# Grouped-query scores with each head's keys standing twice: two full-height products per block

## The chip, the cores and the metric

The kernel runs as one launch on one core of one Trainium2 chip. The metric is device time in microseconds (us); lower is better. Times of several runs are compared by their median, and one further execution was taken with the hardware profiler.

## What is computed

Two layers of a hybrid trunk are run for two groups of tokens with shared weights: 128 context tokens, and 256 latent tokens that also read a cache of 128 context keys. Each layer mixes tokens in three branches (grouped-query attention, latent attention, a recurrent block), merges them by gates and an output projection, and ends in a convolutional feed-forward part. The part that matters here, cut from the reference:

```
qa = rmsnorm(qa.reshape(B, T, H_A, HD_A), lp['g_qa'])     # 8 heads of 64
ka = rmsnorm(ka.reshape(B, T, KV_A, HD_A), lp['g_ka'])    # 2 heads of 64
if cache is not None:                                     # latent tokens
    qa, ka = axial_rope(qa, ang_a), axial_rope(ka, ang_a)
    ka_all = jnp.concatenate([ck, ka], axis=1)            # 128 cached keys, 256 own
...
s = jnp.einsum('bqkgd,bskd->bkgqs', qblk, k, preferred_element_type=jnp.float32) * scale
p = jax.nn.softmax(s, axis=-1).astype(v.dtype)
return jnp.einsum('bkgqs,bskd->bqkgd', p, v)
```

Everything is float32. The kernel gets that precision from a faster matmul type by splitting an operand into a high part (`hi`, rounded to that type) and a low part (`lo`, the rest) and adding the products hi hi, hi lo and lo hi.

## The kernel before

All 384 tokens (128 context, 256 latent) go through a layer together, as three tiles of 128 tokens. `layer_items` writes out by hand, layer by layer, a list of items; an item is one step of TensorE with at most one unit of weights (128 rows by up to 1024 columns). The weights stream through a ring: SP's queue loads a unit into `RAW`, ScalarE writes its high part to `WH`, VectorE the low part to `WL`, and the item's products use both. The order of the items in a layer is: keys and values (`kva`), queries (`qa`), eight steps of the recurrent branch (`xr`, `yr`, `gl`, `wg`), latent attention's projections (`ckr`, `qb`), the recurrent projection (`oc`), `uv` and `uk`, then gates with the two attention projections (`gl`, `oa`, `ob`), in layer 0 with units of the modulation spread among them, then `out`, the feed-forward part (`gat`, `val`, `dn`) and further modulation. An `xr`, `yr` or `gl` item has 24 products of 384 columns.

Work that isn't tied to an item is put on a list `side` of small steps with a budget each; every item pops some of them (`BUDGET`). The eight grouped-query heads are a list of events (`events_a`), of which two are taken behind each `oc` item (`EVENTS`): scores of a head, normalisation, transposes of the probabilities, and for every second head the product with the values. `events_b` does the same for the latent heads among the `gl`, `oa` items.

The instructions so taken down are not issued in that order. `Plan` notes for each what it has to wait for, prices it (`cost`; a product by its columns, whatever its rows), and a list scheduler makes the order of each engine in up to 12 sweeps. Each engine then runs its instructions in that order. All are issued from one line, L371, so the profile's rows carry that line and have to be told apart by tile and shape. `FA` is a float32 area, `RA` the area of the split operands, `PS` the eight PSUM banks.

Keys of the grouped-query heads (`kt`, one side step of a layer, behind the last `kva` item): `KA[:, t]` holds 128 tokens by two key heads of 64. Three transposes put both heads below each other into bank 6 (head 0 in rows 0 to 63, head 1 in rows 64 to 127). Together with the cached keys (`CKC`, loaded already transposed into `FA`) they are written to `KAH` (high part, both heads) and to `KAX[0]` and `KAX[1]`: `KAX[g]` has the low part in the rows of head g and a copy of the high part of the same head in the other 64 rows. Bank 6 is later one of the seven that the `xr`, `yr`, `gl` and `wg` items take in turn; the fourth of those items takes it.

Queries (`q` in `events_a`): for a pair of heads a tile `QTH` or `QTL` holds for one head the high part in that head's 64 rows and the low part in the other 64.

Scores of a head (`s(n)`, `att_scores`): three blocks of queries by keys, 128x384, 128x128 and 128x384, in banks 3 and 4. Each is a sum of two products that are issued next to each other: one over the head's 64 rows (hi hi) and one over all 128 rows (hi lo and lo hi at once). So a head has six products, of alternating height. The latent heads use three products of 96 rows for each block (`mm3`) instead.

Of the kernel before, what the change touches and what calls it, by code (L numbers as in the profile page):

```python
# [14 lines left out]
D = 1024  # L15
# [4 lines left out]
NT = 384                    # columns: 128 context tokens, 256 latent tokens  # L20
TOK = (0, 128, 256)         # first column of each token tile
SEQS = ((0, 128), (128, 256))  # first column and length of each sequence
# [4 lines left out]
WIDTH = 1024                # columns of a weight unit  # L27
NRAW, NW = 4, 4             # units loaded, units split
NPEND = {"out": 8, "dn": 4}  # units whose products wait for the last of them and then go tile by tile
# [4 lines left out]
# per-feature parameters, one column per 128 features  # L34
# [16 lines left out]
# ---------------------------------------------------------------- order of the weights  # L51
QUARTERS = ("q0", "q1", "q2", "q3")     # parts of the first modulation, by features
NARROW = QUARTERS + ("g0", "g1", "h0", "h1")   # parts of 512 columns; halves of the first gate, quarters of the second modulation
# [5 lines left out]
ADDED = ((0, 'g0'), (0, 'g1'), (0, 'h0'), (0, 'h1'), (0, 'm2b'), (1, 'm1a'), (1, 'm1b'), (1, 'gt1'), (1, 'm2b'))   # (layer, part) whose products are added up before the sum over the partitions  # L59
# [9 lines left out]
def fill(items, extra):  # L69
    """extra spread evenly over items"""  # L70
    out, n, k = [], len(items), 0
    for i, it in enumerate(items):
        out.append(it)
        while k < len(extra) and (k + 1) * n <= (i + 1) * len(extra):
            out.append(extra[k])
            k += 1
    return out + extra[k:]
# [11 lines left out]
def layer_items(l):  # L89
    """Every entry is one step of the tensor engine with at most one unit of weights, in order."""  # L90
    more = l + 1 < DEPTH
    s = [("kva", l, k) for k in range(2)] + [("qa", l, k) for k in range(4)]
    if l == 0:                                                  # half of the features while the other's modulation is on its way
        s = ada(0, "q0") + [("norm1", 0, 0)]
        for q in range(1, 4):
            b = ada(0, QUARTERS[q])
            s += [("kva", 0, q - 1)] + b[:2] + [("qa", 0, q - 1)] + b[2:] + [("norm1", 0, q)]
        s += [("kva", 0, 3), ("qa", 0, 3)]
# [57 lines left out]
# ---------------------------------------------------------------- the order of the instructions  # L156
# [4 lines left out]
class Plan:  # L161
    """Takes down instructions in an order that is right, and hands them to the engines in one that keeps them busy.

    An instruction comes behind those whose results it reads, and those whose operands or results it overwrites.
    Of the others an engine gets the one that is waited for soonest; the order in which the tensor engine's were
    taken down sets the pace."""
# [18 lines left out]
    # ---- taking down  # L185
    @staticmethod
    def spans(ap):
        """[(first, last word)] and the partitions that an access pattern covers"""
# [41 lines left out]
    def add(self, eng, method, f, args, kw):  # L230
# [20 lines left out]
        if tab:                                                 # the functions that need a table stay in order  # L251
# [14 lines left out]
    def depend(self, op, outs, ins):  # L266
        before = {}
        for write, aps in ((False, ins), (True, outs)):
            for ap in aps:
                self.touch(op.i, ap, write, before)  # L270
                if ap.space == bass.MemoryType.PSUM:            # the engines take turns at a bank
# [6 lines left out]
        if op.eng == "PE":                                      # accumulations of a bank stay in order  # L278
# [6 lines left out]
    def join(self):  # L285
        """what is taken down inside goes to its engine in one piece"""
# [5 lines left out]
    def touch(self, me, ap, write, before):  # L292
        """notes what ap covers; before[op]: whether me has to wait for op's end"""
# [16 lines left out]
    # ---- handing out  # L310
    def lag(self, p, s):
        """from the end of p to the first start of s"""
# [6 lines left out]
    def sweep(self, rank, back):  # L319
        """starts of all instructions, each engine taking the ready one of the lowest rank; in reversed time if back"""  # L320
# [27 lines left out]
    def order(self):  # L348
        ops = self.ops
        now, rank = 0.0, [None] * len(ops)  # L350
        for op in ops:                                          # the pace of the tensor engine
            if op.eng == "PE":
                rank[op.i] = now
                now += op.dur
# [23 lines left out]
# ---------------------------------------------------------------- the kernel  # L378
def trunk(tc, I, O, depth=DEPTH):
    nc = tc.nc  # L380
    with tc.tile_pool(name="sb", bufs=1) as sb, tc.tile_pool(name="ps", bufs=1, space=bass.MemoryType.PSUM) as pp:
        def t(name, shape, dtype=F32):
# [7 lines left out]
            NST=t("NST", [16]), SM=t("SM", [256]), XS=tc.dram_tile([3, 128, D], F32, name="x_spill"),  # L390
# [8 lines left out]
def _emit(plan, G, V, A, PE, SP, I, O, depth, B):  # L399
    PS, FA, RA, HH, HL, RAW, WH, WL = (B[k] for k in ("PS", "FA", "RA", "HH", "HL", "RAW", "WH", "WL"))  # L400
    PARM, PAR, GV, CST, CS, MOD, GEV, RG, NST, SM, XS, AS, ONE = (
        B[k] for k in ("PARM", "PAR", "GV", "CST", "CS", "MOD", "GEV", "RG", "NST", "SM", "XS", "AS", "ONE"))
# [22 lines left out]
    # ---- addresses  # L425
# [8 lines left out]
    KAH, KAX = ra(9264, 512), [ra(9776 + 512 * i, 512) for i in range(2)]  # L434
# [16 lines left out]
    CKC = fa(11286, 128)  # L451
# [48 lines left out]
    def rsq_few(v, n):  # L500
        """v ** -0.5 for a few columns"""
# [15 lines left out]
    # ---- the stream of weights  # L517
# [7 lines left out]
    spare = {}                                                  # places of split units beside the ring's  # L525
# [50 lines left out]
    def on_gpsimd(u):  # L576
        """units that are split where VectorE is behind"""
# [22 lines left out]
    def take():  # L600
        """the next unit: (hi, lo), or what was loaded for one that isn't split"""
# [46 lines left out]
    # ---- constants  # L648
# [20 lines left out]
    def rnn_constants():  # L669
# [4 lines left out]
        # z = exp(-|lam|): 2 ** -k times a series  # L674
# [16 lines left out]
        # log1p(z) = 2 atanh(z / (2 + z))  # L691
# [14 lines left out]
    # ---- modulation  # L706
# [89 lines left out]
    def alpha_build(l, which):  # L796
        """AL[:, i] = 32 (gate_i + bias) g_post, on all partitions"""
# [11 lines left out]
    # ---- norms  # L809
# [3 lines left out]
    def rstd(ss, eps):  # L813
        """(D * (mean + eps)) ** -0.5 from the sums of two halves"""
# [35 lines left out]
    def post_half(t, h, ss):  # L850
        """what half of out needs before its norm is known"""
# [9 lines left out]
    # ---- token-major projections of attention  # L861
# [12 lines left out]
    def headnorm(banks, dst, heads, g):  # L874
        """steps to dst[t] = rmsnorm of the first heads*64 columns of each bank, rotated for the latents"""
# [40 lines left out]
    # ---- attention  # L916
# [42 lines left out]
    def heads(q, s, pv, per):  # L959
        """steps of the eight heads, each between two items"""  # L960
# [17 lines left out]
    def events_a():  # L978
        def q(p):
# [3 lines left out]
            for q, h, o in ((QTH[p % 2], LOW, HIGH), (QTL[p % 2], HIGH, LOW)):   # hi in the head's rows, lo in the other's  # L983
# [4 lines left out]
        def s(n):  # L988
            q, h = ((QTH, LOW), (QTL, HIGH))[n % 2]
            q, x = q[(n // 2) % 2], KAX[n % 2]  # L990

            def product(out, q0, k0, w):                                # hi hi, then hi lo and lo hi in one
                with plan.join():
                    PE.matmul(out, lhsT=q[h, q0:q0 + 128], rhs=KAH[h, k0:k0 + w], start=True, stop=False)
                    PE.matmul(out, lhsT=q[:, q0:q0 + 128], rhs=x[:, k0:k0 + w], start=False, stop=True)
# [15 lines left out]
    # ---- recurrent branch  # L1011
    def tap(y, b, w, d):
        """adds w times the column d further on, within each sequence"""
# [70 lines left out]
    # ---- the walk over the items  # L1084
# [11 lines left out]
    def require(key):  # L1096
        """the step of that name is behind us"""
# [11 lines left out]
    def do(it):  # L1109
# [29 lines left out]
        elif kind == "kva":  # L1139
            k0 = it[2]  # L1140
            if k0 == 0:
# [3 lines left out]
                SP.dma_start(out=CKC, in_=I["ckT"][l])  # L1145
# [6 lines left out]
            if k == KD - 1:  # L1152
# [4 lines left out]
                def kt():  # L1157
                    for t in range(3):
                        PE.transpose(PS[:, 6, 128 * t:128 * t + 128], KA[:, t], IDN)
# [407 lines left out]
```

## Time and profile before

| what | value |
|---|---|
| time, median of 3 runs | 1491.57 us |
| the three runs | 1489.84, 1491.57, 1496.32 us |
| span of the profiled execution | 1487.3 us |
| TensorE products (PE), busy | 1441.8 us, 97% |
| TensorE weight loads (PEld), busy | 1322.3 us, 89% |
| VectorE (DVE), busy | 1089.1 us, 73% |
| ScalarE (ACT), busy | 823.5 us, 55% |
| GpSimd (POOL), busy | 89.4 us, 6% |
| granted TensorE clock, mean | 0.991 of full speed |
| read from memory | 219.40 MB, 150 GB/s over the span |

The span runs from the first to the last instruction of the profiled execution; the profile gives no other time of that execution. Busy times of the engines overlap. TensorE's products are pipelined: the profile's duration of one (0.33 us for 384 columns) holds its whole way through the array, so the distance from one start to the next is what a product costs in a stream. Rows with the operation LDWEIGHTS, engine PEld, are the loads of the stationary operand that precede each product. Shapes such as 64*128 64x384 mean: a stationary operand of 64 rows by 128 columns, a moving one of 64 rows by 384 columns.

### The profile page before, as it was taken

Reading aid. Unit: us, or ns where it says so; the run is one execution under the profiler, and the core shown is the slowest. Engines: PE = TensorE matmul, PEld = TensorE weight load, DVE = VectorE, ACT = ScalarE, POOL = GpSimd, SP = SyncE. Lnnn points to the kernel's source line nnn. Section 1 sums busy time; section 2 is a strip of 40 time slices with the busy share of each in tenths; the row PEclk is TensorE's granted clock in tenths of the full one; section 3 lists DMA queues with packets and bytes.
Section 4 is the critical chain, followed back from the end, with each engine's and each line's share of the span. In section 5 each row is a group of like instructions: output and inputs, shape, how many; then the busy total and the mean of one; then the engine's idle time right before and its main releaser. Section 6 shows DMA issues by size and latency. Waiting matters only on the chain.

```text
span 1487.3 us, 22398 instructions
## 1 busy us (share of the span) xinstructions
PE 1441.8 (97%) x8408; PEld 1322.3 (89%) x8408; DVE 1089.1 (73%) x2150; ACT 823.5 (55%) x1450; POOL 89.4 (6%) x70
## 2 busy tenths in 40 slices
PE   7999999999898999999989999999999999999998
PEld 5999988988786999997769999979999879999886
DVE  3989896898586798988768787966556477777533
ACT  4689965766335554452255799646544455454321
POOL 0000000334002000000020000000000200000000
PEclk9999999999999999999999999999999999999999
DMA  9433331445674554547754333412246364433341
GB/s 362 165 122 121 122 124 53 131 170 160 214 262 170 172 193 147 173 153 251 243 205 137 124 121 110 127 59 75 87 148 206 126 205 124 127 125 126 128 128 57
DMA packets 79101, 225.11 MB, mean 151 GB/s; under 512 B 9808, under 2 KB 21648, under 8 KB 78992
## 3 DMA queue, kind: packets, MB, share of 16 engines
q1 hardware_dynamic: 68576, 216.04, 43.6%
q10 hardware_dynamic: 10416, 7.64, 2.0%
q8 instruction: 66, 1.08, 0.3%
q14 instruction: 43, 0.35, 0.1%
HBM read 219.40 MB, written 4.24 MB: 150 GB/s over the span
## 4 chain that ended last, share of the span: by engine, by line
PE 85%; DVE 5%; DMA 5%; issue 2%; ACT 1%; ACTq 0%; SPq 0%; POOL 0%; DVEq 0%; POOLq 0%
PE PS L371 85%; DMA RAW<-in_wstream_dram 4%; DVE FA L371 3%; DVE WL L371 1%; ACT FA L371 1%; DMA FA<-in_wstream_dram 0%; ACT WH L371 0%; DMA a_spill<-FA 0%; DVE SM L371 0%; DVE RA L371 0%; ACTq L371 0%; SPq L371 0%; POOL SM L371 0%; ACT RA L371 0%; DVE MOD L371 0%
## 5 line engine op out<-in xcount | busy, mean ns | idle before, releaser
L371 DVE TENSOR_TENSOR WL<-RAW,WH 128x1024 fp32r<-128x1024 f32 (+4 forms) x318 | 351.3, 1107 | 173.1 <-ACT WH L371 172.1
L371 ACT ACTIVATE WH<-RAW 128x1024 fp32r<-128x1024 f32 (+3 forms) x328 | 311.3, 954 | 261.3 <-PE PS L371 218.2
L371 PE MATMUL PS<-HH,WH 128*128 128x384 f32 x1344 | 452.7, 337 | 0.5 <-DVE FA L371 0.4
L371 PE MATMUL PS<-HL,WH 128*128 128x384 f32 x1344 | 450.0, 335 | 0.8 <-DVE HL L371 0.8
L371 PE MATMUL PS<-HH,WL 128*128 128x384 f32 x1344 | 449.8, 335 | 0.0
L371 PEld LDWEIGHTS PS<-HH,WH 128*128 128x128 f32 x1344 | 253.0, 188 | 3.6 <-issue 2.8
L371 PEld LDWEIGHTS PS<-HL,WH 128*128 128x128 f32 x1344 | 252.8, 188 | 1.5 <-DVE HL L371 1.2
L371 PEld LDWEIGHTS PS<-HH,WL 128*128 128x128 f32 x1344 | 252.7, 188 | 0.0
L371 PE MATMUL PS<-WH,RA 128*128 128x512 f32 x608 | 196.7, 395 | 0.0
L371 PE MATMUL PS<-RA,WH 128*128 128x384 f32 (+1 forms) x672 | 181.5, 351 | 9.3 <-ACT FA L371 9.3
L371 ACT ACTIVATE FA<-PS 128x384 f32<-128x384 f32 (+4 forms) x180 | 98.9, 559 | 144.1 <-PE PS L371 141.6
L371 DVE SCALAR_TENSOR_TENSOR FA<-PS,PAR,FA 128x255 f32<-128x255 f32 (+1 forms) x448 | 155.7, 409 | 10.0 <-ACT FA L371 9.9
L371 PEld LDWEIGHTS PS<-WH,RA 128*128 128x128 f32 x608 | 114.7, 189 | 27.1 <-issue 1.2
L371 PEld LDWEIGHTS PS<-RA,WH 128*128 128x128 f32 x672 | 119.7, 191 | 12.5 <-ACT FA L371 10.7
L371 DVE SCALAR_TENSOR_TENSOR FA<-RAW,CS,FA 128x1024 f32<-128x1024 f32 (+1 forms) x98 | 115.6, 1202 | 11.1 <-DMA RAW<-in_wstream_dram 10.8
L371 PE MATMUL PS<-WL,RA 128*128 128x512 f32 x304 | 119.9, 394 | 0.0
L371 PE MATMUL PS<-RA 128*128 128x512 f32 (+4 forms) x456 | 113.3, 374 | 2.0 <-DVE RA L371 1.6
L371 PE MATMUL PS<-RA,WL 128*128 128x384 f32 (+1 forms) x336 | 115.0, 342 | 0.0
L371 ACT ACTIVATE FA<-PS,PAR 128x384 f32<-128x384 f32 x168 | 101.9, 629 | 20.5 <-PE PS L371 20.1
L371 DVE TENSOR_TENSOR FA<-FA 128x384 f32<-128x384 f32 (+3 forms) x213 | 105.8, 509 | 3.3 <-ACT FA L371 1.5
L371 PEld LDWEIGHTS PS<-RA 128*128 128x128 f32 (+2 forms) x456 | 80.1, 188 | 28.9 <-issue 13.3
L371 ACT ACTIVATE FA<-FA 128x384 f32<-128x384 f32 (+1 forms) x100 | 54.0, 546 | 67.8 <-DVE FA L371 64.4
(80 smaller groups left out, 1584.8 us busy)
## 6 DMA issues: line engine op xcount, KB each, us to landing
RAW<-in_wstream_dram SPq DMA_DIRECT2D x330, 512.0 KB, 3.6
RAW<-in_wstream_dram SPq DMA_DIRECT2D x52, 256.0 KB, 3.1
FA<-in_wstream_dram SPq DMA_DIRECT2D x22, 512.0 KB, 7.0
RAW<-in_wstream_dram SPq DMA_DIRECT2D x16, 384.0 KB, 3.6
FA<-a_spill ACTq DMA_DIRECT2D x16, 256.0 KB, 9.7
FA<-in_x_dram SPq DMA_DIRECT2D x6, 512.0 KB, 5.2
RAW<-in_wstream_dram SPq DMA_DIRECT2D x8, 288.0 KB, 2.7
x_spill<-FA ACTq DMA_DIRECT2D x3, 512.0 KB, 2.6
```

What stands on the lines that cost most here:

```text
L371: f(*args, **kw)
```

## The change

Each key head now stands twice, one copy below the other, in all 128 rows: `K1[g]` is the high part of head g's keys in both halves, `K2[g]` the low part in both halves. A block of scores is the sum of two products over 128 rows with the same stationary operand: with `K1` it gives hi hi and lo hi, with `K2` hi lo and lo lo (which was left out before).

To get there, a new step `kd` on VectorE writes `KA` with each head doubled into a new tile `KAD` (three copies of 256 columns). The transposes of a layer become six, three for each key head (`kt(0)`, `kt(1)`), both through bank 6. The eviction of a pass is three splits over 128 rows (a ScalarE copy and a VectorE subtraction each) instead of the nine ScalarE and six VectorE instructions for both heads before. The cached keys are doubled on the host and loaded into a tile of their own, `CKT`, 128 KB instead of 64 KB per layer. The budgets of the side steps become 0.6, 1.0 and 1.0 instead of 1.5. The two new tiles take 4 KB of each partition, and the kernel is built with a smaller scratch for dynamic transfers. Queries, softmax and the products with the values stay as they are.

```diff
+            ... CKT=t("CKT", [256]), KAD=t("KAD", [3, 256]), ...
...
-    KAH, KAX = ra(9264, 512), [ra(9776 + 512 * i, 512) for i in range(2)]
+    K1 = [ra(9264 + 512 * i, 512) for i in range(2)]
+    K2 = [ra(10288 + 512 * i, 512) for i in range(2)]
...
-    CKC = fa(11286, 128)
+    CKC = CKT.rearrange("p (g n) -> p g n", g=2)
...
         def s(n):
-            q, h = ((QTH, LOW), (QTL, HIGH))[n % 2]
-            q, x = q[(n // 2) % 2], KAX[n % 2]
+            q, g = (QTH, QTL)[n % 2][(n // 2) % 2], n % 2
             def product(out, q0, k0, w):
                 with plan.join():
-                    PE.matmul(out, lhsT=q[h, q0:q0 + 128], rhs=KAH[h, k0:k0 + w], start=True, stop=False)
-                    PE.matmul(out, lhsT=q[:, q0:q0 + 128], rhs=x[:, k0:k0 + w], start=False, stop=True)
+                    PE.matmul(out, lhsT=q[:, q0:q0 + 128], rhs=K1[g][:, k0:k0 + w], start=True, stop=False)
+                    PE.matmul(out, lhsT=q[:, q0:q0 + 128], rhs=K2[g][:, k0:k0 + w], start=False, stop=True)
...
-                SP.dma_start(out=CKC, in_=I["ckT"][l])
+                SP.dma_start(out=CKT, in_=I["ckT"][l])
...
-                def kt():
+                def kd():
                     for t in range(3):
-                        PE.transpose(PS[:, 6, 128 * t:128 * t + 128], KA[:, t], IDN)
-                    for src, o, n in ((PS[:, 6, 0:128], 0, 128), (PS[:, 6, 128:384], 256, 256), (CKC, 128, 128)):
-                        hi = KAH[:, o:o + n]
-                        A.activation(out=hi, in_=src, func=AF.Copy)
-                        for x, h, other in ((KAX[0], LOW, HIGH), (KAX[1], HIGH, LOW)):
-                            V.tensor_tensor(out=x[h, o:o + n], in0=src[h], in1=f(hi[h]), op=ALU.subtract)
-                            A.activation(out=x[other, o:o + n], in_=src[h], func=AF.Copy)
+                        V.tensor_copy(KAD[:, t].rearrange("p (g s d) -> p g s d", g=2, s=2),
+                                      KA[:, t].rearrange("p (g d) -> p g d", g=2).unsqueeze(2).to_broadcast([128, 2, 2, 64]))
+
+                def kt(g):
+                    for t in range(3):
+                        PE.transpose(PS[:, 6, 128 * t:128 * t + 128], KAD[:, t, 128 * g:128 * g + 128], IDN)
+                    for src, o, n in ((PS[:, 6, 0:128], 0, 128), (PS[:, 6, 128:384], 256, 256), (CKC[:, g], 128, 128)):
+                        split(K1[g][:, o:o + n], K2[g][:, o:o + n], src)
...
-                side.append((1.5, kt))
+                side.extend([(0.6, kd), (1.0, lambda: kt(0)), (1.0, lambda: kt(1))])
...
-    nc = bacc.Bacc("TRN2", target_bir_lowering=False, num_devices=1)
+    nc = bacc.Bacc("TRN2", target_bir_lowering=False, num_devices=1, dynamic_dma_scratch_size=1024)
```

## Rows read from the trace of the kernel before

**Rows 1.** The page: span, TensorE's busy time, the chain that ended last.

```profile
span 1487.3 us, 22398 instructions
...
PE 1441.8 (97%) x8408; PEld 1322.3 (89%) x8408; DVE 1089.1 (73%) x2150; ACT 823.5 (55%) x1450; POOL 89.4 (6%) x70
...
PE 85%; DVE 5%; DMA 5%; issue 2%; ACT 1%; ACTq 0%; SPq 0%; POOL 0%; DVEq 0%; POOLq 0%
```

**Rows 2.** Busy time by stretch: length, engines, granted clock, share and rate of transfers.

```profile
198.00:258.00 60.00, 60.00 (x338) 48.76 (x337) 45.02 (x106) 34.97 (x84) 1.36 (x1) 1.00 0.25 83
260.00:400.00 140.00, 127.53 (x805) 116.68 (x804) 107.72 (x191) 80.92 (x156) 42.21 (x27) 0.96 0.50 162
...
946.00:1004.00 58.00, 58.00 (x326) 47.03 (x326) 43.23 (x103) 31.44 (x74) 0.00 (x0) 1.00 0.24 79
1004.00:1220.00 216.00, 211.77 (x1248) 193.36 (x1248) 126.69 (x235) 111.80 (x219) 14.23 (x10) 0.98 0.45 142
```

**Rows 3.** Timeline of TensorE's products at layer 0's first score block: start, length, instructions.

```profile
197.27 0.51 PE L371 MATMUL PS<-RA,WH 128*128 128x384 f32 x2
...
197.79 0.51 PE L371 MATMUL PS<-RA,WH 128*128 128x384 f32 x2
198.15 0.33 PE L371 MATMUL PS<-RA,WL 128*128 128x384 f32 x1
198.41 2.06 PE L371 MATMUL PS<-RA 64*128 64x384 f32 x6
200.31 0.57 PE L371 MATMUL PS<-RA,WH 128*128 128x384 f32 x2
200.72 0.34 PE L371 MATMUL PS<-RA,WL 128*128 128x384 f32 x1
```

**Rows 4.** Timeline of the weight loads in that block; in brackets idle time before.

```profile
198.41 0.18 PEld L371 LDWEIGHTS PS<-RA 64*128 64x128 f32 x1 [0.25 <-ACT FA L371]
198.78 0.19 PEld L371 LDWEIGHTS PS<-RA 128*128 128x128 f32 x1 [0.19 <-issue]
```

**Rows 5.** Timeline of TensorE's products at a latent head's score block in layer 0.

```profile
269.30 1.55 PE L371 MATMUL PS<-RA 96*128 96x384 f32 x9
270.68 0.52 PE L371 MATMUL PS<-RA,WH 128*128 128x384 f32 x2
```

**Rows 6.** TensorE's groups by form: count, busy us, mean ns.

```profile
L371 PE MATMUL PS<-RA 64*128 64x384 f32 x32 | 14.0, 439 | 0.0
```

**Rows 7.** Timeline of TensorE: starts of the fifth, sixth and eighth block.

```profile
231.58 0.81 PE L371 MATMUL PS<-RA 64*128 64x384 f32 x2
...
237.54 0.80 PE L371 MATMUL PS<-RA 64*128 64x384 f32 x2
...
252.48 0.81 PE L371 MATMUL PS<-RA 64*128 64x384 f32 x2
```

**Rows 8.** Timeline of the key transposes in layer 0 and their last eviction.

```profile
56.74 0.49 PE L371 MATMUL PS<-CST,FA 128*128 128x128 f32 x3
56.98 0.42 PE L371 MATMUL PS<-HH,WH 128*128 128x384 f32 x1
...
63.03 0.38 ACT L371 ACTIVATE RA<-PS 64x256 fp32r<-64x256 f32 x1 [0.49 <-DVE RA L371]
```

**Rows 9.** VectorE's groups by form: subtractions of 256 columns over 64 and 128 rows.

```profile
L371 DVE TENSOR_TENSOR RA<-PS,RA 64x256 fp32r<-64x256 f32 x4 | 1.7, 419 | 0.2
L371 DVE TENSOR_TENSOR RA<-PS,RA 128x256 fp32r<-128x256 f32 x4 | 1.6, 409 | 0.0
```

**Rows 10.** The chain that ended last, in layer 0: start, length, what.

```profile
91.27 200.41 PE PS L371 x1176
...
381.73 11.52 DMA RAW<-in_wstream_dram
```

**Rows 11.** Load of the cached keys (tile view), and busy time early on.

```profile
L371 SPq DMA_DIRECT2D FA<-in_ckT_dram x2: 327/384/440, 46.1 to 782.2; - x2
...
20.00:40.00 20.00, 19.74 (x230) 15.76 (x227) 11.06 (x37) 8.86 (x20) 0.00 (x0) 1.00 0.97 366
```

More of the change, by code (lines that the diff above doesn't have):

```diff
@@ L389, in trunk @@
             CS=t("CS", [KD, 32]), ONE=t("ONE", [2, 32]), MOD=t("MOD", [DEPTH, 4, 2, KD]), GEV=t("GEV", [256]), RG=t("RG", [2, DEPTH * 16]),
-            NST=t("NST", [16]), SM=t("SM", [256]), XS=tc.dram_tile([3, 128, D], F32, name="x_spill"),
+            NST=t("NST", [16]), SM=t("SM", [256]), CKT=t("CKT", [256]), KAD=t("KAD", [3, 256]), XS=tc.dram_tile([3, 128, D], F32, name="x_spill"),
             AS=tc.dram_tile([2 * DEPTH, 128, 256], F32, name="a_spill"))
@@ L400, in _emit @@
     PS, FA, RA, HH, HL, RAW, WH, WL = (B[k] for k in ("PS", "FA", "RA", "HH", "HL", "RAW", "WH", "WL"))
-    PARM, PAR, GV, CST, CS, MOD, GEV, RG, NST, SM, XS, AS, ONE = (
-        B[k] for k in ("PARM", "PAR", "GV", "CST", "CS", "MOD", "GEV", "RG", "NST", "SM", "XS", "AS", "ONE"))
+    PARM, PAR, GV, CST, CS, MOD, GEV, RG, NST, SM, XS, AS, ONE, CKT, KAD = (
+        B[k] for k in ("PARM", "PAR", "GV", "CST", "CS", "MOD", "GEV", "RG", "NST", "SM", "XS", "AS", "ONE", "CKT", "KAD"))
     stt = {"pend": []}
@@ L1534, in layout @@
         cv=np.ascontiguousarray(a["cache_gqa_v"][0].reshape(DEPTH, 128, 128)),
-        ckT=np.ascontiguousarray(a["cache_gqa_k"][0].reshape(DEPTH, 128, 128).transpose(0, 2, 1)),
+        ckT=np.ascontiguousarray(np.repeat(a["cache_gqa_k"][0].reshape(DEPTH, 128, 2, 64).transpose(0, 2, 3, 1)[:, :, None], 2, 2)
+                                 .reshape(DEPTH, 2, 128, 128).transpose(0, 2, 1, 3)).reshape(DEPTH, 128, 256),
         ccT=np.ascontiguousarray(a["cache_mla_ckv"][0].reshape(DEPTH, 128, 2, 128).transpose(0, 3, 2, 1)),
```

## Prediction

> **What bounds the kernel now.** I read the page first, then the busy time by stretch, then the instructions of the score blocks in order of time, then the group of score products by form, and last the chain through layer 0.
>
> The page says that TensorE is busy 97% of a span of 1487.3 us and that 85% of the chain that ended last is its own products [rows 1]. That is an average, so the stretches of the change are to be read by themselves. The eight grouped-query heads of layer 0 lie between 198 and 258 us and those of layer 1 between 946 and 1004 us. In both TensorE has no idle time at all (60.00 of 60.00, 58.00 of 58.00), at a granted clock of 1.00, its 2.4 GHz level, while VectorE is busy 75% and ScalarE 58% and 54% [rows 2]. A busy TensorE is not one at its pace, though. What the reader should look at is the distance between starts.
>
> In the stream of weight products three products of 384 columns take 0.52 us (197.27 to 197.79), so 0.175 us each. The score block of the first head starts at 198.41, holds six products (four of 384 columns, two of 128) and is followed at 200.31 by the next weight product: 1.90 us [rows 3]. The weight loads of the same stretch show why: the first load has 64 rows, the next 128, they stand 0.37 us apart, and before the second the loader was idle 0.19 us with nothing that the profile shows to wait for [rows 4]. Products and loads normally overlap; here each load waits until the array has finished with the other height.
>
> The latent-attention scores of the same kernel are the control. Their block has nine products (six of 384, three of 128 columns), all 96 rows high, and takes 1.38 us from 269.30 to 270.68 [rows 5]. Six by 0.175 is 1.05, which leaves 0.33 for three of 128 columns, 0.11 each. So products of one height run at the pace of their columns, and the alternation of 64 and 128 rows is what stretches the other block. Nine products take less time than six.
>
> **The change part by part.**
>
> *Scores.* All products of a block become 128 rows high, in number and columns as before. By the prices just read a block then takes 4 x 0.175 + 2 x 0.11 = 0.92 us: 0.98 us less than 1.90. There are 32 products of 64x384 [rows 6], two in a block, so 16 blocks: 15.7 us. To this come the borders. From the last weight product to the first score product there are 0.26 us (198.15 to 198.41) for a product of 0.175, 0.085 lost; the two weight products behind the block take 0.41 us (200.31 to 200.72) for 0.35, another 0.06 [rows 3]. Some blocks have a border beside transposes, or beside value products of 64 columns that keep a switch of their own, or are split in two by other work. So I bound the borders by one of 0.085 and both of 0.145 a block, 1.4 to 2.3 us for 16, and take 1.7, near the middle. Sum: 17.4 us less TensorE time, 8.7 in each layer, bounds 17.1 to 18.0.
>
> A switch costs some 0.19 us on a product of 384 columns by the rows. The Trainium skill, page TensorEngine Tiling, section Key Properties, says that a change of tiling mode drains the engine; it has no price for it, and by the constant of a lone warm product on the page TensorE: Matmul & The Clock Gate, section Single matmul latency (166 ns), the six changes of height in each of 16 blocks would come to an estimate of 15.9 us. The trace agrees with the drain, at 0.19 us instead of 0.166, and its sum stands.
>
> *Does the rest of the head keep up?* Blocks start at 198.41 and, the eighth, at 252.48 [rows 3, 7], 7.7 us apart on average, of which 5.8 us is other TensorE work that stays. The closest pair starts at 231.58 and 237.54 [rows 7], so with a block of 1.9 us the maxima, exponentials and normalisation of one head fitted into 4.1 us. Only the blocks shrink, so that pause stays 5.8 on average. VectorE's 45.0 us of the 60 [rows 2] would then stand in 51.3, 88%: not yet the bound.
>
> *Keys.* Per layer there are three more transposes. The three of before stand at 56.74, and the stream goes on at 56.98: 0.24 us [rows 8]. Twice that is 0.5 us, and with a border of 0.1 for each second pass I take 0.7 us; bounds 0.5 to 1.7 (the latter with a pause like 0.19 before each of six). Of the evictions, nine ScalarE and six VectorE instructions become six and six. Half the rows cost as much as all: 0.42 us for 64x256, 0.41 for 128x256 [rows 9]. So VectorE's share stays, ScalarE loses three copies, and VectorE gains three doubling copies of 256 columns. Nothing in the trace is such a copy; below is nothing, which the work excludes, above a two-operand instruction of 0.41 us; I take 0.41, 1.2 us per layer. All of this hides behind the xr and yr products, at which TensorE does not wait. The cover: the keys' last eviction of bank 6 ends at 63.4 [rows 8], and the next product in that bank comes two items of 24 products behind 56.98, at 56.98 + 2 x 4.2 = 65.4. That leaves 2.0 us. The second pass of transposes now waits for the first one's evictions from the same bank. From 56.98 to 63.4 us ten evictions of the bank took 6.4 us among other work; eight of them and one more turn of about a microsecond (a transpose's 0.24 and an eviction's 0.4, with their handing on) is much the same. If the cover goes, the fourth item's products wait, and all behind them on TensorE; a pass of 3 us in each layer would cost 6 us.
>
> *Load of the cached keys.* It doubles to 128 KB, and its own tile frees it of the wait that put it at 46.1 us [rows 11]. It may now go into the start, where the transfers already fill the engines at 366 GB/s [rows 11]: 131 KB by that rate is 0.36 us, bounds 0 and 0.4; I take nothing, since the weight loads of the start have earlier due times. The smaller scratch of dynamic transfers and the two tiles are memory only.
>
> *What comes next.* In layer 1 nothing stands in the way: up to 1220 us TensorE is busy 211.8 of 216 us and VectorE 59% [rows 2]. In layer 0 the chain is TensorE without a break from 91.27 on for 200.41 us, then leaves it for VectorE and transfers (one landing took 11.52 us at 381.73) [rows 10]; TensorE idles 12.5 of the 140 us from 260 to 400 [rows 2]. That stretch starts from TensorE's results, VectorE is busy 77% in it, so it should move up as a whole. I let a tenth of layer 0's gain be lost there.
>
> Net: 17.4 - 0.7 = 16.7, less 0.8 = 15.9 us. The profiled span is 1487.3, so the span after should be 1471.4. The profile gives no other time of that execution; the median of the runs is 4.3 us above it, which I take as staying: 1491.57 - 15.9 = 1475.7 us.
>
> **Rivals.**
>
> *Layer 0's gain is waited off.* If VectorE or the ring of weights paces 260 to 480 us by itself, TensorE only arrives earlier and waits longer. For it: the chain leaves TensorE there. Against: VectorE's 23% idle. The gain is layer 1's: 8.35 us, 1483.2.
>
> *The pause isn't from the heights.* Then the time goes by columns alone, nothing is gained, and the transposes cost 0.7: 1492.3. For it: the two products of a block share their queries, which could make one load wait for the other. Against: the latent block's first two products share theirs too, and it runs at full pace [rows 5]. The Trainium skill, page TensorE: Matmul & The Clock Gate, section Why this matters for your kernels, says a low product takes the time of a full one. That holds between products of one height, 96 rows in 0.175 us; in alternation the trace differs, 0.37 us.
>
> *Slower: the order is made anew.* Every instruction is placed by a list scheduler, and a few new ones can shift the order everywhere. The place where that would hurt is layer 0's modulation stretch, where a transfer queued behind others landed after 11.52 us [rows 10]. From 15.9 us of such waits on the gain is gone, from 23.4 us on the kernel is slower by over 0.5%: two more waits of that size give 1498.7, three 1510.3. For it: TensorE idles only there. Against: the scheduler's costs go by columns, so the score products look the same to it before and after, and the real ones come closer to its plan. By the same mechanism the order can also turn out better, by half of those 12.5 us: 1469.5.
>
> **How the numbers follow.** A measurement of this kernel can tell about 0.5%, 7.5 us, from no change: faster is below 1484.1, slower above 1499.0. The forecast (1472 to 1480) has 0.66, layer 0 waited off (1480 to 1484) 0.14, a better order 0.06: faster 0.86. No gain, or one eaten by a late bank 6 or one long transfer: 0.10. Slower 0.04. The range reaches from the better order, 1469, to layer 0 waited off, 1484; what is left out is the 0.14 of same and slower and part of the better orders. Unknown costs (borders 0.6, transposes 1.0, the load 0.4) lie inside it.
>
> **What would show it.** The form 64x384 is gone, and 64 products of 128x384 and 32 of 128x128 stand in its place; a score block takes 0.9 to 1.0 us from its start to the next product; the pause of 0.19 before each load is gone. The stretch from the first to the eighth block of layer 0 falls from 54.1 to about 47 us. Layer 1 must show at least 8 us by 1004. I am wrong if blocks stay above 1.5 us, if TensorE idles in the score stretches, or if the idle time between 260 and 480 us has grown by what the blocks gave.

## The result, and the profile after

Medians: 1493.06 us before (1489.84 to 1496.32, 4 runs), 1476.88 us after (1473.47 to 1480.59, 4 runs). The ratio is 0.990 [0.987, 0.992], a gain of 16.2 us where 15.9 were forecast; the time lies 1.2 us above the forecast. Two later comparisons gave 0.990 [0.988, 0.993] and 0.993 [0.990, 0.995].

The page of the kernel after: the span, the busy times of the engines, and the chain by engine.

```profile
span 1478.8 us, 22419 instructions
PE 1429.6 (97%) x8414; PEld 1325.0 (90%) x8414; DVE 1087.9 (74%) x2156; ACT 822.2 (56%) x1444; POOL 89.3 (6%) x70
...
PE 82%; DVE 6%; DMA 6%; ACT 2%; issue 2%; ACTq 1%; POOL 0%; SPq 0%; DVEq 0%; POOLq 0%
```

TensorE still has 97% of the span [rows 1], now 12 us less of it, and the chain has moved a little towards VectorE and transfers. The profiled spans differ by only 8.5 us (1487.3 and 1478.8), the medians by 16.2: the profiled execution of after was its slowest, 1480.59 us. The score blocks first: TensorE's products and then its weight loads at layer 0's second block, the counterpart of [rows 3, 4].

```profile
205.25 0.35 PE L371 MATMUL PS<-RA,WL 128*128 128x384 f32 x1
205.43 1.03 PE L371 MATMUL PS<-RA 128*128 128x384 f32 x6
206.29 0.57 PE L371 MATMUL PS<-RA,WH 128*128 128x384 f32 x2
```

```profile
205.25 1.07 PEld L371 LDWEIGHTS PS<-RA 128*128 128x128 f32 x6
206.24 0.30 PEld L371 LDWEIGHTS PS<-RA,WH 128*128 128x128 f32 x2
```

From start to start the block takes 0.86 us (205.43 to 206.29); six loads stand in one row, with no pause between them. The groups by form:

```profile
L371 PE MATMUL PS<-RA 128*128 128x384 f32 x64 | 15.1, 347 | 0.0
L371 PE MATMUL PS<-RA 128*128 128x128 f32 x32 | 5.4, 251 | 0.0
L371 PE MATMUL PS<-CST,KAD 128*128 128x128 f32 x12 | 2.1, 272 | 0.0
L371 DVE COPY KAD<-FA 128x256 f32<-128x256 f32 x6 | 1.5, 284 | 0.0
```

The 64 and 32 products are the forms that the prediction named. The last two groups are the six transposes of each layer (three before) and the doubling copies, 284 ns each. Then the windows of after that answer to [rows 2], placed by the same work:

```profile
197.00:249.00 52.00, 51.87 (x338) 48.17 (x337) 45.38 (x106) 34.31 (x80) 1.38 (x1) 1.00 0.27 89
260.00:400.00 140.00, 124.15 (x774) 114.72 (x773) 107.03 (x186) 77.86 (x150) 41.02 (x27) 0.94 0.50 158
...
945.00:994.00 49.00, 49.00 (x322) 45.45 (x322) 41.83 (x102) 31.80 (x75) 0.00 (x0) 1.00 0.30 95
994.00:1212.00 218.00, 213.29 (x1256) 194.79 (x1255) 127.84 (x238) 112.45 (x219) 14.35 (x10) 0.98 0.44 140
```

Layer 0's score stretch holds its 338 products in 52 us instead of 60, layer 1's about as many in 49 instead of 58. VectorE is busy 87% and 85% in them: close, and still not the bound. In the stretch to 400 us TensorE's idle time has risen from 12.5 to 15.9 us and its mean granted clock fallen from 0.96 to 0.94. There stands the long pause of layer 0; TensorE's products around it, the number in brackets being the idle time before:

```profile
383.58 0.34 PE L371 MATMUL PS<-HH,WL 128*128 128x384 f32 x1
393.05 1.01 PE L371 MATMUL PS<-RA,WH 128*128 128x384 f32 x2 [9.13 <-ACT FA L371]
```

Before, the same pause was 7.35 us long and ended at 394.76. The chain of after leads into it, where [rows 10] had a transfer of 11.52 us at 381.73; `a_spill` is a scratch area in DRAM into which ScalarE's queue writes a result and from which it reads it back:

```profile
362.48 7.10 DMA a_spill<-FA
...
376.66 14.87 DMA RAW<-in_wstream_dram
...
393.05 4.02 PE PS L371 x12
```

One more pause is new in all three traces of after, early in layer 0:

```profile
103.93 0.34 PE L371 MATMUL PS<-RA,WL 128*128 128x384 f32 x1
105.67 0.45 PE L371 MATMUL PS<-HH,WH 128*128 128x384 f32 x1 [1.40 <-ACT FA L371]
```

The starts of TensorE's work on its way through the two profiled executions, in us (a ledger of the 8.5 us):

| | before | after | after minus before |
|---|---|---|---|
| first score block, layer 0 | 198.41 | 197.59 | -0.8 |
| eighth score block, layer 0 | 252.48 | 246.23 | -6.3 |
| end of the long pause | 394.76 | 393.05 | -1.7 |
| first score block, layer 1 | 946.62 | 945.72 | -0.9 |
| eighth score block, layer 1 | 1000.66 | 992.40 | -8.3 |
| end of the span | 1487.3 | 1478.8 | -8.5 |

In this execution layer 1's gain goes through to the end, and layer 0's is largely given back at the pause. The two other traces of after differ: there the eighth block of layer 1 comes 11.4 us earlier than before, but the spans are only 7.9 and 8.5 us shorter, because TensorE waits later in layer 1, for 3.78 and 3.25 us at 1121 us. The trace above has 1.66 us there, that of before nothing over 0.7, and a run with low products in layer 1 (below) has 4.95. So this pause doesn't need an early arrival; what makes it was not tried.

### The profile page after: what moved, and what is told of

It reads as the page before. It is cut to its first block, busy times and chain, and to the rows that moved or that the text cites. A ratio compares the mean times of both kernels' runs of the same rounds, so it can differ in the third digit from the quotient of the medians.

```text
span 1478.8 us, 22419 instructions
## 1 busy us (share of the span) xinstructions
PE 1429.6 (97%) x8414; PEld 1325.0 (90%) x8414; DVE 1087.9 (74%) x2156; ACT 822.2 (56%) x1444; POOL 89.3 (6%) x70
## 4 chain that ended last, share of the span: by engine, by line
PE 82%; DVE 6%; DMA 6%; ACT 2%; issue 2%; ACTq 1%; POOL 0%; SPq 0%; DVEq 0%; POOLq 0%
PE PS L371 82%; DMA RAW<-in_wstream_dram 5%; DVE FA L371 4%; DVE WL L371 1%; ACT FA L371 1%; DMA a_spill<-FA 1%; ACT WH L371 1%; DVE RA L371 1%; ACTq L371 1%; DMA FA<-in_wstream_dram 0%; DMA FA<-in_rows_dram 0%; ACT L371 0%; DVE SM L371 0%; ACT RA L371 0%; POOL SM L371 0%
## 5 line engine op out<-in xcount | busy, mean ns | idle before, releaser
L371 PE MATMUL PS<-RA,WH 128*128 128x384 f32 (+1 forms) x672 | 182.2, 352 | 13.7 <-ACT FA L371 13.7
L371 PEld LDWEIGHTS PS<-RA,WH 128*128 128x128 f32 x672 | 120.1, 191 | 17.1 <-ACT FA L371 14.9
L371 PE MATMUL PS<-RA 128*128 128x512 f32 (+4 forms) x456 | 97.6, 356 | 1.6 <-DVE RA L371 1.6
L371 PEld LDWEIGHTS PS<-RA 128*128 128x128 f32 (+1 forms) x456 | 78.5, 189 | 13.0 <-DVE RA L371 2.3
```

The lines of the kernel that those rows point to most:

```text
L371: f(*args, **kw)
```

## The experiments

**Theories.** H: the time lay in the changes of height between 64 and 128 rows, and only there. K: it lay in the new keys, in other evictions or in the order that the scheduler made of them. Beside them stood the question of what becomes of layer 0's gain (W: it is waited off at the pause).

**The new keys with low products.** The first product takes the head's 64 rows again; the order of the instructions on each engine is that of after, instruction for instruction in the two traces.

```diff
+            h = (LOW, HIGH)[g]
-                    PE.matmul(out, lhsT=q[:, q0:q0 + 128], rhs=K1[g][:, k0:k0 + w], start=True, stop=False)
+                    PE.matmul(out, lhsT=q[h, q0:q0 + 128], rhs=K1[g][h, k0:k0 + w], start=True, stop=False)
```

> The changed kernel with one thing undone: the first product of each block covers the head's 64 rows again (lo hi is left out of the scores); keys, doubling, transposes and the order of every engine stay those of the changed kernel. If the alternation of heights is the cause, score blocks are back at 1.90 us and the 17.4 us come back: a ratio to the kernel before of 1.000 to 1.003 (about 1490 to 1497 us). If the new keys or the new order brought the gain, it stays: ratio 0.988 to 0.992.

Measured: 1.001 [1.000, 1.003], nothing gained. TensorE at the second block, the long form back:

```profile
206.76 2.05 PE L371 MATMUL PS<-RA 64*128 64x384 f32 x6
208.65 0.56 PE L371 MATMUL PS<-RA,WH 128*128 128x384 f32 x2
```

The block takes 1.89 us. K is out.

**The old keys with full products.** The other corner: the kernel before, in its own order, with only the height changed. Its scores carry a term of the other head, so it serves for its time alone.

```diff
-                    PE.matmul(out, lhsT=q[h, q0:q0 + 128], rhs=KAH[h, k0:k0 + w], start=True, stop=False)
+                    PE.matmul(out, lhsT=q[:, q0:q0 + 128], rhs=KAH[:, k0:k0 + w], start=True, stop=False)
```

> The kernel before with one thing changed: the first product of each block covers all 128 rows, with the keys of both heads as they stand (so the scores carry a foreign term); keys, transposes and the order of every engine stay those of the kernel before. Heights as cause: blocks of 0.92 us, the whole gain of some 17 us: ratio 0.987 to 0.990 (1473 to 1479 us). Keys or order as cause: ratio 0.998 to 1.002. Against the changed kernel it should be 0.7 us faster by the price of the second pass of transposes, too little to be told apart.

Measured: 0.989 [0.987, 0.991]. TensorE at its second block, 0.86 us:

```profile
203.75 1.03 PE L371 MATMUL PS<-RA 128*128 128x384 f32 x6
204.61 0.39 PE L371 MATMUL PS<-RA,WH 128*128 128x384 f32 x1
```

So height alone gives the whole gain in either order. The third kernel of this comparison was after once more:

> The changed kernel once more, beside the others on one chip: ratio 0.988 to 0.992 by both theories. It gives the spread of the same program and whether layer 0's late stall (9.3 us before 393 us) is the program's or the execution's: if the program's, the same stalls within 1 us; if the execution's, they differ by several.

It gave 0.990 [0.988, 0.993], and its long pause was 8.83 us, within 1 us of 9.13. That spoke for the program's own pause; two traces of the version with zeros (below) have 6.24 and 9.97 us, so one execution alone doesn't size it.

**Two changes of height in a block.** Before, with its six products in the order high, high, low, low, low, high instead of alternating (the three blocks of a product are collected, then issued):

```diff
+            blocks = []
...
+                    for (o_, q0, k0, w), full, first in ((wide, 1, 1), (last, 1, 1), (wide, 0, 0), (small_, 0, 1), (last, 0, 0), (small_, 1, 0)):
```

> The kernel before with the six products of a head in another sequence, high, high, low, low, low, high, so that the height changes twice instead of six times; same products, same keys. If each change of height costs 0.19 us (0.145 on 128 columns), a block holds 0.92 + 2 x 0.19 = 1.3 us with its borders and 11 us of the 17 come back: ratio 0.991 to 0.994. If a low product is slow by itself (0.37 us each, the high ones not), half comes back, 8 us: ratio 0.994 to 0.996, and the low products stand 0.37 us apart. If something else stretches the block, 1.000.

Measured: 0.994 [0.991, 0.996]. The loads in one block, idle time in brackets:

```profile
206.08 0.37 PEld L371 LDWEIGHTS PS<-RA 128*128 128x128 f32 x2
...
206.70 0.47 PEld L371 LDWEIGHTS PS<-RA 64*128 64x128 f32 x3 [0.25 <-issue]
...
207.36 0.19 PEld L371 LDWEIGHTS PS<-RA 128*128 128x128 f32 x1 [0.18 <-issue]
```

Three low loads follow one another without a pause; the two pauses stand where the height changes. A block loses about 0.4 us instead of 1.1, 11 us less in 16 blocks; 11.3 were measured by the medians (1490.2 and 1478.95), 9.7 by the ratio. The interval of the ratio reaches into both ranges expected, so it is the trace that decides. A low product is not slow: the change is.

**96 rows.** After, with the even heads' first product over 96 rows instead of 128; the odd heads keep 128.

```diff
+            h = (slice(0, 96), slice(0, 128))[g]
-                    PE.matmul(out, lhsT=q[:, q0:q0 + 128], rhs=K1[g][:, k0:k0 + w], start=True, stop=False)
+                    PE.matmul(out, lhsT=q[h, q0:q0 + 128], rhs=K1[g][h, k0:k0 + w], start=True, stop=False)
```

> The changed kernel with the first product of every even head over 96 rows instead of 128 (part of lo hi left out there), the odd heads as they are: 96 and 128 rows alternate. If any change of height costs a pause, the even heads' blocks return to 1.9 us and 8.5 us are lost: ratio 0.995. If 96 rows run in the array's full height and only 64 do not, blocks stay at 0.87 to 0.97 us and the ratio at 0.990.

Measured: 0.989 [0.987, 0.991]. TensorE at one such block:

```profile
238.62 1.05 PE L371 MATMUL PS<-RA 96*128 96x384 f32 x6
239.50 0.41 PE L371 MATMUL PS<-CST,FA 128*128 128x128 f32 x2
```

0.88 us, where the same block of after takes 0.87: 96 and 128 rows alternate at the pace of the columns. A difference of height is not enough; of the heights tried, only 64 beside 128 costs.

**The gain in one layer alone.** After, with the low first product kept in the other layer:

```diff
+            h = (LOW, HIGH)[g] if stt['l'] == 1 else slice(0, 128)
...
+                    stt['l'] = l
```

> The mirror image: full height in layer 0, 64-row first products in layer 1 (lo hi left out there). If layer 0's transfers near 380 us hold up what arrives early, about 2 us of its 8.7 are lost there: a gain of 6.5 to 7 us, ratio 0.9955 to 0.997 and TensorE's long pause before 390 us at 9 us or more instead of 7.4. If layer 0 passes everything on, 8.7 us and a pause of 7.4. If it waits all of it off, 0 to 1 us and a pause of 16.

> The changed kernel with 64-row first products (lo hi left out) in layer 0 alone, full height in layer 1; the order of every engine is that of the changed kernel. Layer 1 has nothing behind its score stretch that waits, so its 8.7 us of shorter blocks should all arrive: 0.9942 of the kernel before (0.9955 if measured from the all-alternating run, which stood at 1.0013). Rival, that layer 1 also loses some of it in its late transfers: under 6 us.

Measured: gain in layer 0 alone 0.998 [0.996, 0.999]; in layer 1 alone 0.997 [0.996, 0.998]. Both gave less than expected (0.9955 to 0.997, and 0.9942 or 0.9955). The long pause in the two traces, layer 0 alone first:

```profile
390.11 1.01 PE L371 MATMUL PS<-RA,WH 128*128 128x384 f32 x2 [10.06 <-ACT FA L371]
```

```profile
396.36 1.01 PE L371 MATMUL PS<-RA,WH 128*128 128x384 f32 x2 [7.92 <-ACT FA L371]
```

With low products in layer 0 the pause ends at 396.36 here and at 396.11 in the first experiment; with full ones there at 390.11, 6 us earlier, of 8.1 us that had arrived at the last latent block (349.4 against 341.3). In this pair W holds for about a quarter: the work in front comes earlier, the pause grows by 2 us. These are single executions, though. The trace with 96 rows, which gains as much in layer 0, has a pause of 7.88 us that ends at 387.52, 8.6 us earlier, and lost next to nothing.

**Zeros in the unused rows.** Before, with 64 rows of zeros in a tile of high parts, so that full-height products add nothing. It needs no doubled keys and no second pass of transposes, but two GpSimd fills and three more ScalarE copies per layer.

```diff
-    KAH, KAX = ra(9264, 512), [ra(9776 + 512 * i, 512) for i in range(2)]
+    KZ, KAX = [ra(9264 + 512 * i, 512) for i in range(2)], [ra(10288 + 512 * i, 512) for i in range(2)]
...
+                    G.memset(f(KZ[0][HIGH]), 0.0)
+                    G.memset(f(KZ[1][LOW]), 0.0)
```

> A version in place of both: keys transposed once as before, but the high part of each key head stands in its own 64 rows with zeros in the other 64, so that both products of a block cover 128 rows; no doubling, no second pass of transposes, no lo lo; ScalarE has three key copies more per layer than before and GpSimd two fills. Its order is nearly that of the kernel before. Heights as cause: blocks of 0.92 us and a ratio of 0.987 to 0.991, equal to the run with full rows and old keys and 0.7 us below the changed kernel by the transposes; if the changed kernel's order costs 1.6 us more at 104 us, 2 to 3 us below it. If zeros or ScalarE's copies cost, it stays above 0.991.

> The version with zeros once more, beside the changed kernel on one chip. If saving the second pass of transposes and the changed kernel's stall of 1.6 us at 104 us shows in the time, it is 1 to 3 us below the changed kernel (ratio 0.988 to 0.990); if not, the two are the same within 0.15%.

Measured: 0.991 [0.989, 0.993], and again 0.992 [0.989, 0.994] beside after's 0.993 [0.990, 0.995] of the same comparison. Both stand at the limit of 0.991 that was set for a cost of the zeros or the copies, and their intervals leave that open. The medians lie 2.9 us apart (1474.92 and 1477.81), but the intervals overlap, so the 1 to 3 us expected were not resolved. Its traces lack the pause at 105 us.

The kernel after ran a third time beside this and the next two:

> The changed kernel a third time, as the partner of the others on this chip: ratio 0.989 to 0.991.

**The plan told how long the spill takes.** The transfer into the spill, early in the chain above, is planned with 2 us for its landing and took 5.7 to 7.1 us in three traces of after. In these two kernels its landing alone is planned at 7 us; nothing else is edited, and the scheduler makes a new order.

```diff
+        op.spill = op.dma and outs[0].tensor.name.startswith("a_spill")
-            return self.DMA_LAT
+            return 7000 if p.spill else self.DMA_LAT
```

> The changed kernel with one number of the scheduler changed: it now counts 7 us instead of 2 us for the landing of the gate's spill (the traces show 5.8 to 7.1 us), so it should give ScalarE other work while that is on its way. If layer 0's pause before 390 us comes from ScalarE standing behind the spill, with the weight copy and the next load behind it, the pause falls from 9 us to below 5 and the ratio to the kernel before to 0.985 to 0.988. If the pause comes from the slow landing of the weight loads themselves (13 to 15 us there), it stays at 8 to 10 us and the ratio at 0.990. A new order can also cost up to a few us by itself.

> The version with zeros and the same number changed. By the first theory 3 to 5 us below the version with zeros, a ratio of 0.985 to 0.988; by the second 0.989 to 0.991.

Measured: on after, 1468.81 us (1464.78 to 1470.63, 5 runs), 0.987 [0.984, 0.990], below every run of after in that comparison (1473.14 to 1480.61); on the zeros, 1469.65 us, 0.989 [0.986, 0.992], against an expected 0.985 to 0.988, and 5.3 us below the zeros of that comparison, against 3 to 5. The pause in the first (lines count one more there):

```profile
384.54 1.01 PE L372 MATMUL PS<-RA,WH 128*128 128x384 f32 x2 [5.05 <-ACT FA L372]
```

It is 5.05 instead of 9.48 us (the zeros: 3.38, from 6.24 and 9.97). ScalarE in front of it, the third trace of after first; `ACTq` rows are transfers that ScalarE's queue issues, here the reads back from the spill:

```profile
368.79 3.96 ACTq L371 DMA_DIRECT2D FA<-a_spill  x4
372.86 1.06 ACT L371 ACTIVATE WH<-RAW 128x1024 fp32r<-128x1024 f32 x1 [8.74 <-DMA FA<-a_spill]
...
388.88 1.06 ACT L371 ACTIVATE RA<-RAW 128x1024 fp32r<-128x1024 f32 x1 [13.12 <-DMA RAW<-in_wstream_dram]
```

```profile
366.82 1.06 ACT L372 ACTIVATE WH<-RAW 128x1024 fp32r<-128x1024 f32 x1 [3.56 <-PE PS L372]
...
368.08 2.89 ACTq L372 DMA_DIRECT2D FA<-a_spill  x4
...
382.64 1.06 ACT L372 ACTIVATE RA<-RAW 128x1024 fp32r<-128x1024 f32 x1 [8.50 <-DMA RAW<-in_wstream_dram]
```

The copy of the weights now stands ahead of the reads back, and the load that waits for it is issued at 369.17 instead of 375.20. The load itself is as slow as it was, 13.4 us for 13.7. So the first theory holds for the start of the load, and its slowness stays. In these two traces 5.2 us are won by the first score block of layer 1 (937.37 and 942.52), and the spans are 10.2 us apart; the rest stands behind that layer's scores, where the pause at 1121 us is missing. There the order is almost the same, so that half is not shown to be the plan's. This kernel has the lowest median, 9 us (0.6%) below after in the same comparison; the zeros with the same number can't be told from it.

**All kernels at one clock.** TensorE's mean granted clock differs from run to run of one kernel; all runs lie between 0.985 and 0.995. Over the 146 runs of all kernels a run's span falls by 1.1 us for each 0.001 of clock, within a kernel. Mean span, and the span put at a clock of 0.990 by that slope:

| kernel | runs | mean span | mean clock | at 0.990 |
|---|---|---|---|---|
| before | 53 | 1487.3 | 0.9899 | 1487.2 |
| low products, new keys | 12 | 1490.2 | 0.9889 | 1489.0 |
| full products, old keys | 6 | 1471.2 | 0.9883 | 1469.3 |
| two changes of height | 6 | 1477.6 | 0.9887 | 1476.1 |
| after (three comparisons) | 18 | 1474.6 | 0.9891 | 1473.5 |
| 96 rows | 4 | 1471.0 | 0.9905 | 1471.6 |
| zeros | 12 | 1473.5 | 0.9887 | 1472.0 |
| full in layer 0 only | 12 | 1483.9 | 0.9876 | 1481.1 |
| full in layer 1 only | 12 | 1481.7 | 0.9894 | 1481.0 |
| after, plan with 7 us | 5 | 1466.8 | 0.9918 | 1468.8 |
| zeros, plan with 7 us | 6 | 1468.5 | 0.9908 | 1469.4 |

So put, height is worth 17.9 us in the old order and 15.5 in the new; new keys with low products cost 1.8; and the layers give 7.9 and 8.0, together 15.9 against the 15.5 of both. By the ratios alone, each against that of low products with new keys, the layers gave about 5.7 and 6.7 us and did not seem to add up. This is a regression, not an experiment: no run set the clock by itself. The clock is also partly an outcome, as it falls in TensorE's long pause (last section), so the last column can take out part of what a pause costs. By the mean spans as they stand, height is worth 16.1 and 15.6 us, and the layers give 6.3 and 8.5, together 14.8.

## Why the prediction was right

*The scores: right.* The six changes of height per block were the cost. The forecast was 17.4 us. Counted from start to start, TensorE lost 17.4 us in the 16 blocks of before against the pace of its columns and 0.5 in those of after: 16.9 back. The blocks of after take 0.86 to 1.01 us; 0.92 was forecast. The page TensorEngine Tiling of the Trainium skill, section Key Properties, says that a change of tiling mode drains TensorE. The trace agrees for 64 and 128 rows: in the grouped order the pauses stand at the changes alone (0.25 and 0.18 us). 96 beside 128 rows showed none.

*The stretch in layer 0: size off.* From first to eighth block it fell from 54.1 to 48.6 us, not to about 47. With the new order and low products it is 55.7, with the old order and full products 46.7: height takes off 7.1 and 7.3, as forecast, and the stretch is 1.6 to 1.9 us longer in the new order at either height. The rest of the head kept up: TensorE was busy 51.87 of 52 us.

*Layer 1: right up to 1004 us.* At least 8 us were asked; its eighth block comes 8.3 us earlier than before (0.9 of them from layer 0, and 0.9 more come within the block), and with the order held, the stretch from its first block to its last latent block is 8.4 us shorter (141.8 and 133.4). That nothing stands in the way behind it was read from one trace; the pause at 1121 us takes 3 us in two of the three traces of after.

*Transposes, copies, cover, load: right in sum.* TensorE at the two passes of after, and the last eviction of bank 6 by VectorE, the counterpart of [rows 8]:

```profile
55.45 0.49 PE L371 MATMUL PS<-CST,KAD 128*128 128x128 f32 x3
55.70 0.42 PE L371 MATMUL PS<-HH,WH 128*128 128x384 f32 x1
...
60.49 0.49 PE L371 MATMUL PS<-CST,KAD 128*128 128x128 f32 x3
60.74 0.42 PE L371 MATMUL PS<-HH,WH 128*128 128x384 f32 x1
```

```profile
62.32 0.42 DVE L371 TENSOR_TENSOR RA<-PS,RA 128x256 fp32r<-128x256 f32 x1
```

Each pass takes 0.25 us (0.5 together, 0.7 with borders forecast); a copy takes 0.28 us for 0.41; the bank is free at 62.74 instead of 63.41, so its cover held. The load of the cached keys left the start alone (tile view, issue times at the end: 45.4 and 84.7 us):

```profile
L371 SPq DMA_DIRECT2D CKT<-in_ckT_dram x2: 327/380/433, 45.4 to 84.7; - x2
```

*The order made anew: a price that was set at nothing.* The pause of 1.40 us at 105 us stands in every kernel with the doubled keys and in none with the old ones or the zeros. TensorE waits there for ScalarE, which loads a table for 1.28 us (ACT_TABLE_LOAD at 103.83) just ahead of the result; before, the same load stood at 102.16 and nothing waited. What in the new order makes ScalarE late was not tried. The 1.8 us of the low products with new keys, beyond 0.5 us of transposes, answers to it. It was a rival's mechanism (the order) at a small size.

*Layer 0's loss: mis-sized.* Set at a tenth, 0.8 us. TensorE's idle time between 260 and 480 us rose from 18.8 to 21.7 us (19.7 and 20.3 in the other traces of after): by 1 to 3 us, far from the 8 that would have refuted the forecast. The pause, 7.35 us before and 7.18 in the same order with low products, is 9.13, 8.83 and 9.48 in three traces of after; it ends 3.1, 6.4 and 5.7 us earlier than with low products. Of 7.9 to 8.4 us arriving, 2 to 5 are lost there, 2 in the layer's own experiment and next to nothing in the trace with 96 rows. What waits there is shown: the spill and then a transfer of weights, 13.0 to 14.9 us on its way in after, 11.4 to 12.1 with low products in layer 0. That an earlier start makes this transfer itself longer was not tested by itself and stays open: the version with zeros starts it early and has 10.4 and 14.2 us in its two traces.

*Span and time: wrong, without harm.* I took 4.3 us around the span. Every run with both numbers shows 1.8 (1.7 to 1.9), so the profiled execution of before took about 1489.1 us (1487.3 + 1.8) and lay below the three listed runs; the 2.5 us left of the 4.3 were spread between runs and no fixed part. Against a forecast of 15.9 the three comparisons gave 16.2, 14.5 and 10.7 us; about half of the difference between the last two goes with the clock. Over all runs the gain is 12.7 us by the mean spans and 13.7 at equal clock. So the forecast lies 2 to 3 us above the gain, about the size of the two terms above, and that the first comparison came within 0.3 us of it is luck. One slip among the rivals: two more waits of 11.52 us are 23.0 us, short of the 23.4 from which the kernel counted as slower, and three give 1510.2 us.

## What to carry to other kernels

Read the distance from start to start, not the busy time, where products of different heights stand beside each other: at 97% busy and full clock TensorE lost 17 us here. Give low products 128 rows (with zeros, or terms that are wanted anyway), or put those of one height behind one another, which brought back about two thirds here; both are cheap edits. And where a scheduler makes the order, compare the landing times in its plan with the trace: one honest number gave 9 us in its comparison, more than half of what the edit itself brought, and 4.7 at equal clock (1473.5 against 1468.8).

## What the runs showed of the hardware

- The price of a change between 64 and 128 rows: about 0.19 us of an idle loader each time (0.25 and 0.18 in the grouped order), 1.1 us for a block of six products. 96 beside 128 rows costs 0.02 us a block at most. Where the limit lies between 64 and 96 was not tried.
- In the long pause the granted clock falls, and it is still low behind it. Windows of after, the clock being the third number from the end:

```profile
380.00:400.00 20.00, 10.87 (x53) 10.55 (x52) 7.27 (x10) 5.78 (x9) 0.00 (x0) 0.74 0.54 161
380.00:386.00 6.00, 3.92 (x23) 3.60 (x21) 0.00 (x0) 0.00 (x0) 0.00 (x0) 1.00 0.73 159
387.00:396.00 9.00, 2.96 (x9) 2.96 (x10) 3.27 (x6) 4.44 (x7) 0.00 (x0) 0.50 0.35 127
```

0.74 is the mean of two levels, 2.4 GHz (1.00) and 1.2 GHz (0.50); before had 0.83 in the same window, with a pause 1.8 us shorter. TensorE stood idle from 383.92 to 393.05: the clock fell within that time, and the first 3 us of products behind it still ran at 1.2 GHz.
- Runs of one kernel differ by 12 us in span (1467.6 to 1479.4 for after) and more (13.7 for before), and the slower ones tend to have the lower mean clock, in after 0.987 for the slowest against 0.993 for the fastest. Two profiles are compared by their spans only after a look at that number.
